# A hybrid RWKV-7 and NSA layer pair on one core: VectorE's and TensorE's order written down from the first key block to the last gate block

## The chip, the core and the metric

The kernel runs on one NeuronCore of a Trainium2 chip. The metric is device time in microseconds. Five engines have their own instruction streams: TensorE (PE, with its weight loads shown apart as PEld), VectorE (DVE), ScalarE (ACT), GpSimd (POOL) and SyncE (SP), which here only issues DMAs. Times are lower-is-better, and one measurement of this kernel spreads over about 0.2%.

## The reference, cut to what matters

The input is one sequence of 256 tokens with 2048 channels. The first layer is an RWKV-7 mixer, the second an NSA attention layer over a shared key/value projection; a last norm ends it. The change lies in the first layer, in the part that makes keys and gates and prepares the scan:

```python
mixed = u[None] + xx[None] * mu[:, None, None, :]
rkvz = jnp.einsum('nbtd,nde->nbte', mixed[:4], w_rkvz)
r, k, v, z = rkvz[0], rkvz[1], rkvz[2], rkvz[3]
...
decay = jnp.exp(-jnp.exp(w_log.astype(jnp.float32)))
a = jax.nn.sigmoid(a0 + (xa @ a1) @ a2)
kk = heads(k * k_k).astype(jnp.float32)
kk = kk / jnp.maximum(jnp.sqrt(jnp.sum(kk * kk, axis=-1, keepdims=True)), 1e-12)
k = k * (1.0 + (a - 1.0) * k_a)
...
o = wkv7_scan(rh, heads(decay), kh, vh, -kk, kk * ah.astype(jnp.float32))
...
o = (o + bonus.reshape(B, T, D)) * jax.nn.silu(z)
```

The kernel computes the scan in chunks of 64 tokens. For that it needs, per head and chunk, the inverse of a unit lower triangular 64x64 matrix, of which the two 32x32 diagonal blocks are inverted by VectorE (128 of them at once, one per partition, for half of the heads).

## The kernel before, in words

**Products in split precision.** Every weight piece of 512 columns is loaded by SyncE into `wraw`. ScalarE rounds it to the fp32r tile `whi` (`Weights.high`, line 211), VectorE makes the rest `wlo` as raw minus high (`Weights.low`, line 190). Activations are split in the same way into a high and a low half (`split_into`, lines 424 to 428). A product is then three matmuls: high by high, high by low, low by high. In a z block (`rows_step`, lines 577 to 590) one step over 128 input channels is one weight piece and six matmuls of 512 columns, three for each half of the tokens. In a k block (`cols_step`, lines 599 to 610) one weight piece serves four steps of three matmuls of 256 columns. There are five buffers for `whi` and `wlo` (`AHEAD + 2`): when the phase takes piece t, the split of piece t+3 is given, and its buffer is the one that the matmuls of piece t-2 have read.

**The stretch that the change touches.** `ZK` orders it: gate block z 0, sixteen key blocks k 0 to k 15 (`phase_k`), then gate blocks z 1 (`phase_z1`), z 2 and z 3 (`late_z`). After these comes the scan, in which all engines run in an order that a planner (`Deal`) lays out by costs and due times.

**Side stages of a k block.** After step 3 (`KP`) of block j, four small stages are given at once, each for a different earlier block: `k_close(j-3)`, `k_open(j)`, `k_turn(j-2)`, `k_norm(j-1)`. Each begins with a few TensorE products into PSUM: close has 16 small matmuls on `at` and `BK`, both in the tile `sp` (line 765); open has two on the loaded `w2s` (lines 705, 706); turn has two transposes of `rnx` (line 745); norm has four matmuls on the squares `sqk` (line 732). Behind the products come their readers: in close two ScalarE copies and three SyncE stores to `abd`; in open two tanh and a copy on ScalarE, the running sum `cum` on VectorE (line 712), exponentials on ScalarE and a product `an` on GpSimd (line 719); in turn `nk` and `at` on VectorE (lines 750, 751), four GpSimd products into `BK` (line 756) and the store to `spd`; in norm a maximum `sst` on VectorE (line 735), a power on GpSimd (line 736) and the copy `rnx` on ScalarE (line 738). At a block's end `k_square` squares and copies the block's result on ScalarE, and VectorE multiplies `f` (line 726). In z 1 the remaining stages are given after the steps 0, 6 and 12 (`ZP`).

**The inverse.** `stage_t(b)` runs in the background for two halves of the heads. It starts when `k_close(8b+7)` is given, loads the matrices back from `abd` into `invA` (line 812; on SyncE for b = 0, on GpSimd for b = 1), and then gives a serial chain of small VectorE operations (line 824): levels 2 and 4, then sixteen dots of level 8 (a multiply and a reduce each, with ScalarE transposes `Tt` ahead) and eight dots of level 16, then two stores. Half b = 1 begins only when half 0 is given in full. What is left of half 1 at the start of the scan is dealt there by the planner.

**How the order comes about.** The program's generators are interleaved by `Sched`: a phase yields costs, each adds to `sch.t`, and a background generator goes on when `sch.t` has passed the time that it asked for. A k step costs 327, a z step 1,280, and the side stages add their own sums to `sch.t` (720, 410, 215 and 500). The pauses in the inverse are times the factor 1.5 for b = 0 and 2 for b = 1. This gives an order of emission. Inside `tc.manual_schedule(engines=...)` the named engines keep it. All others are ordered by the framework's list scheduler, which takes the order of emission as a priority only and brings an instruction forward when it reckons that it is ready. Before the change, only TensorE keeps the order of emission, from k 0 to the end of z 1. In either case each engine's order is fixed when the program is built.

**The split of r.** After z 1 the sixteen tiles of r (`split_into(..., "r", k)`, VectorE at line 427) are made. So that ScalarE does not begin them early, their copy reads its scale from a one-element tile `gate` that GpSimd fills behind z 1.

Of the kernel before, what the change touches and what calls it, by code (L numbers as in the profile page):

```python
# [70 lines left out]
KPO = 3  # L71
KP, ZP = 3, (0, 6, 12)
AUX = {2: ("B0",), 3: ("G",), 4: ("B1",), 5: ("Y",), 7: ("A0",), 8: ("A1",), 9: ("T",)}
# [151 lines left out]
def hybrid_kernel(ctx: ExitStack, tc: tile.TileContext, a: dict, out: bass.AP):  # L225
# [197 lines left out]

    def split_into(src, nm, k, scale=1.0):
        h, l = ring(nm, k)
        S.activation(h, src, AF.Copy, scale=scale)  # L426
        V.tensor_tensor(l, src, h.bitcast(F32), op=OP.subtract)
        mixed[(nm, k)] = (h, l)
# [118 lines left out]
    def mixgen():  # L547
        for names in (("w", "a"), ("z",), ("k",), ("r",)):
            if names == ("r",):
                for k in range(NK):  # L550
                    x = xx[:, k, :]
                    V.scalar_tensor_tensor(x, x, MU[0][:, k:k + 1], xn[:, k, 1:], op0=OP.mult, op1=OP.add)
                    yield DR0
            for k in range(NK):
                for nm in names:
                    if not ring_free(nm):
                        yield lambda: ring_free(nm)
                    if nm in "wa":
                        while ("v", k) not in mixed:
                            yield 300.0  # L560
                    if nm == "r":
                        if k == 0:
                            yield lambda: "z1" in phase_done
                        split_into(xx[:, k, :], nm, k, gates[1.0])
                    else:
                        mix(nm, k)
                    yield {"w": DW, "a": DW, "k": DK, "z": DZ, "r": DRM}[nm]
        phase_done.add("mixed")
# [82 lines left out]

    gates = {}

    def gate(value):
        t = ph1.tile([128, 1], F32, name="gate", bufs=1)
        G.memset(t, value)
        gates[value] = t

    def close_z(nb, ps, ths, eng):
        for tt in range(2):  # L660
            th = ths[tt]
            S.activation(th, ps[tt], AF.Tanh, scale=gates[0.5] if nb == 1 else 0.5)
            S.activation(th, th, AF.Copy, scale=0.5, bias=0.5)
            V.tensor_tensor(th, ps[tt], th, op=OP.mult)
            store_heads(zd, nb, tt, th, eng)

    def phase_z(nb):
        ps = two()
        yield from rows_block(ps, "z", 512)
        close_z(nb, ps, [kph.tile([128, 512], F32, name="zth", bufs=2) for _ in range(2)], nc.sync)  # L670

# [23 lines left out]
    def k_open(j):  # L695
# [10 lines left out]
        PE.matmul(la[:, 256:], w2t[:, 1, sc:sc + 128], ha, start=True, stop=True)  # L706
        sch.t += 720
        thw, tha, cum = tmp("thw"), tmp("tha"), tmp("cum")
# [12 lines left out]
    def k_square(j, pk):  # L721
        k = KST[j]
        k["ksb"], k["sqk"] = [kph.tile([128, T], F32, name=n, bufs=2) for n in ("ksb", "t1")]
        S.activation(k["sqk"], pk, AF.Square, scale=KK[:, j:j + 1])
        S.activation(k["ksb"], pk, AF.Copy)
        V.tensor_tensor(k["f"], k["ksb"], k["f"], op=OP.mult)

    def k_norm(j):
        k = KST[j]
        k["rn"] = rn = accp("rn")  # L730
        for tt in range(2):
            PE.matmul(rn[:, 256 + 2 * tt:258 + 2 * tt], k["sqk"][:, tt * 128:(tt + 1) * 128], C("bo"), start=True, stop=True)
        sch.t += 410
        sst, rnt = [kph.tile([128, 2, 2], F32, name=n, bufs=2) for n in ("sst", "rnt")]
        V.tensor_scalar(sst, rn[:, 256:260].rearrange("p (a b) -> p a b", a=2), 1e-24, None, op0=OP.max)
        G.tensor_tensor(rnt, sst, half[:, 0:4].rearrange("p (a b) -> p a b", a=2), op=OP.pow)
        k["rnx"] = kph.tile([128, T], F32, name="rnx", bufs=2)
        S.activation(k["rnx"].rearrange("p (a b n) -> p a b n", a=2, b=2),
                     rnt[:, :, :, None].to_broadcast([128, 2, 2, 64]), AF.Copy)

    def k_turn(j):
        k = KST[j]
        rn, sp, an, f, pinv = [k[n] for n in ("rn", "sp", "an", "f", "pinv")]
        for tt in range(2):
            PE.transpose(rn[:, tt * 128:(tt + 1) * 128], k["rnx"][:, tt * 128:(tt + 1) * 128], ident)
        sch.t += 215
        k["BK"] = BK = sp[:, 0:512].rearrange("p (c x t) -> p c x t", c=NCH, x=2)
        k["at"] = at = sp[:, SPW - 256:]
# [10 lines left out]
    def k_close(j):  # L759
        k = KST.pop(j)  # L760
        ab, cd = accp("ab"), accp("ab")
        for c in range(NCH):
            for h in range(2):
                r, o = [slice(64 * i, 64 * i + 64) for i in (h, h ^ (c % 2))]
                PE.matmul((ab, cd)[c % 2][o, c // 2 * 64:c // 2 * 64 + 64], c3(k["at"])[r, c, :], k["BK"][r, c, h, :], start=True, stop=True)
        sch.t += 500
        abs_ = k["abs"] if j < 2 else kph.tile([128, T], F32, name="abs", bufs=2)
        S.activation(abs_[:, 0:128], ab[:, 0:128], AF.Copy)
        S.activation(abs_[:, 128:256], cd[:, 0:128], AF.Copy)
        for c, src, dst in ((0, 0, 0), (2, 0, 64), (2, 64, 0)):  # L770
            n = 64 if c else 128
            nc.sync.dma_start(abd[j, c:c + 2, :, dst:dst + n].rearrange("c k p s -> p (c k) s"),
                              abs_[src:src + n, 64 * c:64 * c + 128].rearrange("p (n s) -> p n s", s=32))
        a1done.add(j)

    def phase_k(j):
# [3 lines left out]
        for q in range(4):  # L780
            for s, cost in enumerate(cols_step(o, "k", q)):
                yield cost
                n = 4 * q + s
                if n == KP:
                    for lag, part in ((3, k_close), (0, k_open), (2, k_turn), (1, k_norm)):
                        if j >= lag:
                            part(j - lag)
            if j == NK - 1:
                used.update(("k", k) for k in range(4 * q, 4 * q + 4))
        k_square(j, o)  # L790

    def phase_z1():
        banks(acc=(2, 3, 0, 1))
        gate(0.5)
        ps = two()
        for k in range(NK):
            yield from rows_step(ps, "z", k, W.get(), 512)
            if k in ZP:
                for lag, part in ((3, k_close), (2, k_turn), (1, k_norm)):
                    j = NK + ZP.index(k) - lag  # L800
                    if j < NK:
                        part(j)
        close_z(1, ps, [kph.tile([128, 512], F32, name="zth", bufs=2) for _ in range(2)], nc.sync)
        gate(1.0)
        phase_done.add("z1")
# [87 lines left out]
    def stage_t(b):  # L893
        yield lambda: (8 * b + 7) in a1done
        A = inverse_load(b)
        if b:
            yield lambda: 0 in tdone
        yield 3000.0 if b else 9000.0
        left = inverse_ops(b, A)
# [34 lines left out]
    def late_z(nb):  # L934
        nonlocal A10, T00, vt, zt
        ps = two()
        for k in range(NK):
            yield from rows_step(ps, "z", k, W.get(), 512)
            if nb == 3:
                used.add(("z", k))  # L940
# [4 lines left out]
            elif k == ZHOOK[0]:  # L945
# [11 lines left out]
                for t in (A10, T00, Yb[0]):  # L957
                    G.memset(t, 0.0)
        close_z(nb, ps, [t.rearrange("p x c d -> p (x c d)") for t in (vt, zt)], G)

# [5 lines left out]
    for nm, i in ZK:  # L966
        if (nm, i) == ("k", 0):
            ordered.enter_context(tc.manual_schedule(engines={PE.engine}))
        sch.run((late_z(i) if i > 1 else phase_z1() if i else phase_z(i)) if nm == "z" else phase_k(i))
        if (nm, i) == ("z", 1):  # L970
            ordered.close()
    phase_done.update(("z", "k"))
# [1071 lines left out]
```

## Time and profile before

| | |
|---|---|
| median of 3 runs | 1145.12 us |
| lowest and highest | 1143.18 and 1145.2 us |
| the profiled execution | 1146.2 us |
| its span, first to last instruction | 1144.4 us |
| mean granted TensorE clock | 0.989 |

The profiled execution's own time is 1.8 us more than its span, for what lies around it, and 1.1 us above the median. In the profile "busy" of TensorE counts from a matmul's start to a modelled end, so that pipelined matmuls overlap; how fast they go is read from the distance of their starts. A line of the timeline gives a start, a duration, the engine, the line of the kernel, the operation with written and read tiles, and how many instructions were merged; in square brackets stands the idle time before it and what ended it.

### The profile page before, as it was taken

Reading aid. Unit: us, or ns where it says so; the run is one execution under the profiler, and the core shown is the slowest. Engines: PE = TensorE matmul, PEld = TensorE weight load, DVE = VectorE, ACT = ScalarE, POOL = GpSimd, SP = SyncE. Lnnn points to the kernel's source line nnn. Section 1 sums busy time; section 2 is a strip of 40 time slices with the busy share of each in tenths; the row PEclk is TensorE's granted clock in tenths of the full one; section 3 lists DMA queues with packets and bytes.
Section 4 is the critical chain, followed back from the end, with each engine's and each line's share of the span. In section 5 each row is a group of like instructions: output and inputs, shape, how many; then the busy total and the mean of one; then the engine's idle time right before and its main releaser. Section 6 shows DMA issues by size and latency. Waiting matters only on the chain.

```text
span 1144.4 us, 24519 instructions
## 1 busy us (share of the span) xinstructions
PE 1107.3 (97%) x8880; PEld 939.5 (82%) x8880; DVE 869.0 (76%) x1806; ACT 716.1 (63%) x1696; POOL 367.2 (32%) x465
## 2 busy tenths in 40 slices
PE   8999999998999999999999999999999999999996
PEld 7778899987778777777778878787889988898786
DVE  6999976689786997768666876674576888988564
ACT  5667688866745456566556766564656666666553
POOL 1400057766252556653010010100333435352212
PEclk9999999998989999999999999999999999999999
DMA  6558878876898958864457758585656453848552
GB/s 218 174 190 236 247 203 256 241 219 208 245 271 255 237 159 247 211 171 134 131 179 234 225 164 284 160 292 167 188 148 162 122 146 102 203 114 278 164 186 106
DMA packets 239033, 225.35 MB, mean 197 GB/s; under 512 B 58053, under 2 KB 185333, under 8 KB 238912
## 3 DMA queue, kind: packets, MB, share of 16 engines
q1 hardware_dynamic: 233472, 216.65, 64.5%
q0 software_dynamic: 5440, 7.14, 2.4%
q8 instruction: 70, 1.15, 0.5%
q14 instruction: 51, 0.42, 0.1%
HBM read 200.48 MB, written 23.10 MB: 195 GB/s over the span
## 4 chain that ended last, share of the span: by engine, by line
PE 77%; DVE 9%; DMA 4%; issue 4%; POOL 3%; ACT 2%; SPq 0%; ACTq 0%; POOLq 0%; DVEq 0%
PE bank L587 12%; PE bank L589 12%; PE bank L586 12%; PE bank L1337 5%; PE bank L611 5%; DVE wlo L190 3%; PE bank L612 3%; PE bank L241 2%; PE bank L605 2%; PE bank L606 2%; PE bank L607 2%; PE bank L1340 2%; PE pair L1359 2%; PE pair L1361 1%; PE pair L1360 1%
## 5 line engine op out<-in xcount | busy, mean ns | idle before, releaser
L190 DVE TENSOR_TENSOR wlo<-wraw,whi 128x512 fp32r<-128x512 f32 (+2 forms) x616 | 447.3, 741 | 162.4 <-ACT whi L211 159.4
L211 ACT ACTIVATE whi<-wraw 128x512 fp32r<-128x512 f32 (+2 forms) x664 | 401.3, 620 | 241.4 <-PE bank L589 93.0
L587 PE MATMUL bank<-wlo,mx 128*128 128x512 f32 (+3 forms) x576 | 217.4, 379 | 7.4 <-DVE wlo L190 6.5
L589 PE MATMUL bank<-whi,mx 128*128 128x512 f32 (+3 forms) x576 | 215.6, 377 | 0.0
L586 PE MATMUL bank<-whi,mx 128*128 128x512 f32 (+3 forms) x576 | 187.9, 379 | 2.1 <-ACT mx L426 0.9
L587 PEld LDWEIGHTS bank<-wlo,mx 128*128 128x128 f32 x576 | 109.4, 190 | 26.2 <-DVE wlo L190 8.5
L586 PEld LDWEIGHTS bank<-whi,mx 128*128 128x128 f32 x576 | 108.4, 190 | 20.0 <-ACT whi L211 1.5
L589 PEld LDWEIGHTS bank<-whi,mx 128*128 128x128 f32 x576 | 109.3, 190 | 16.7 <-POOL mx L1926 0.4
L1337 PE MATMUL bank<-mx,whi 128*128 128x512 f32 x256 | 102.1, 430 | 0.0
L190 POOL TENSOR_TENSOR wlo<-wraw,whi 128x512 fp32r<-128x512 f32 (+2 forms) x48 | 63.0, 1314 | 110.8 <-ACT whi L211 90.1
L611 PE MATMUL bank<-mx,whi 128*128 128x512 f32 x240 | 86.6, 397 | 0.0
L605 PE MATMUL bank<-mx,whi 128*128 128x256 f32 (+1 forms) x288 | 83.0, 288 | 0.3 <-ACT mx L426 0.3
L606 PE MATMUL bank<-mx,whi 128*128 128x256 f32 (+1 forms) x288 | 81.4, 283 | 0.0
L607 PE MATMUL bank<-mx,wlo 128*128 128x256 f32 (+1 forms) x288 | 81.3, 282 | 0.0
L587 PE MATMUL bank<-wlo,kvh 128*128 128x512 f32 x192 | 76.9, 401 | 0.0
L589 PE MATMUL bank<-whi,kvl 128*128 128x512 f32 x192 | 76.1, 396 | 0.0
L612 PE MATMUL bank<-mx,wlo 128*128 128x256 f32 x256 | 70.6, 285 | 0.2 <-DVE wlo L190 0.2
L1340 PE MATMUL bank<-mx,wlo 128*128 128x256 f32 x256 | 70.7, 284 | 0.0
L586 PE MATMUL bank<-whi,kvh 128*128 128x512 f32 x192 | 67.4, 396 | 0.0
L1337 PEld LDWEIGHTS bank<-mx,whi 128*128 128x128 f32 x256 | 48.0, 189 | 10.6
L605 PEld LDWEIGHTS bank<-mx,whi 128*128 128x128 f32 (+1 forms) x288 | 54.2, 188 | 1.3 <-ACT mx L426 0.7
L607 PEld LDWEIGHTS bank<-mx,wlo 128*128 128x128 f32 (+1 forms) x288 | 54.2, 188 | 0.8 <-DVE wlo L190 0.2
(350 smaller groups left out, 2301.9 us busy)
## 6 DMA issues: line engine op xcount, KB each, us to landing
wraw<-in_a_w_rkvz_dram SPq DMA_DIRECT2D x128, 512.0 KB, 5.2
wraw<-in_kv_w_dram SPq DMA_DIRECT2D x48, 512.0 KB, 4.5
wraw<-in_b_w_in_dram SPq DMA_DIRECT2D x40, 512.0 KB, 4.3
wraw<-in_a_w_o_dram SPq DMA_DIRECT2D x32, 512.0 KB, 4.6
wraw<-in_b_w_o_dram SPq DMA_DIRECT2D x32, 512.0 KB, 4.1
spd<-sp SPq DMA_DIRECT2D x16, 642.0 KB, 5.4
wraw<-in_b_w_in_dram SPq DMA_DIRECT2D x24, 384.0 KB, 3.3
spl<-spd SPq DMA_DIRECT2D x14, 642.0 KB, 7.2
```

What stands on the lines that cost most here:

```text
L190: eng.tensor_tensor(lv, src, hv.bitcast(F32), op=OP.subtract)
L211: self.nc.scalar.activation(hv, src, AF.Copy)
L586: PE.matmul(o, mh[:, ts], wh[:, 0, :], start=k == ends[0], stop=False)
L587: PE.matmul(o, mh[:, ts], wl[:, 0, :], start=False, stop=False)
L589: PE.matmul(o, ml[:, ts], wh[:, 0, :], start=False, stop=k == ends[1])
L605: PE.matmul(o, wh[:, s, :], mh, start=k == 0 and first, stop=False, **kw)
L606: PE.matmul(o, wh[:, s, :], ml, start=False, stop=False, **kw)
L607: PE.matmul(o, wl[:, s, :], mh, start=False, stop=k == NK - 1, **kw)
L611: PE.matmul(o, wh[:, s, :], joint[nm, k], start=k == 0, stop=False, **kw)
L612: PE.matmul(o[:, :T], wl[:, s, :], mh, start=False, stop=False, **kw)
L1337: both = lambda: PE.matmul(o, wh[:, s, :], joint["r", k], start=k == 0, stop=k == NK - 1)
L1340: PE.matmul(o[:, :T], wl[:, s, :], mixed["r", k][0], start=False, stop=False)
```

## The change

From k 0 to the end of z 3, TensorE and VectorE both keep the order of emission (before: TensorE alone, and only to the end of z 1). Each side stage becomes a generator with a `yield` between its products and their readers. The products are given after step 3 as before (`begin_parts`), the readers after step 11 (`KS8`, `end_parts`); in z 1 the readers follow their products by two steps. VectorE's multiply of `f` moves from `k_square` to the readers of `k_norm`, one block later. The closing multiply and stores of gate blocks 1 and 2 are given after step 1 (`ZREST`) of the next gate block. The pause between the load and the first operation of half 1 of the inverse goes from 3,000 to 8,000. The sums that open and norm add to `sch.t` go from 720 to 860 and from 410 to 500. The `gate` tile goes.

```diff
-KP, ZP = 3, (0, 6, 12)
+KP, KS8, ZP, ZREST = 3, 11, (0, 6, 12), 1
...
-        S.activation(h, src, AF.Copy, scale=scale)
+        S.activation(h, src, AF.Copy)
...
     def close_z(nb, ps, ths, eng):
         for tt in range(2):
             th = ths[tt]
-            S.activation(th, ps[tt], AF.Tanh, scale=gates[0.5] if nb == 1 else 0.5)
+            S.activation(th, ps[tt], AF.Tanh, scale=0.5)
             S.activation(th, th, AF.Copy, scale=0.5, bias=0.5)
-            V.tensor_tensor(th, ps[tt], th, op=OP.mult)
-            store_heads(zd, nb, tt, th, eng)
+
+        def rest():
+            for tt in range(2):
+                V.tensor_tensor(ths[tt], ps[tt], ths[tt], op=OP.mult)
+                store_heads(zd, nb, tt, ths[tt], eng)
+        return rest
...
-        sch.t += 720
+        sch.t += 860
+        yield
         thw, tha, cum = tmp("thw"), tmp("tha"), tmp("cum")
...
         S.activation(k["ksb"], pk, AF.Copy)
-        V.tensor_tensor(k["f"], k["ksb"], k["f"], op=OP.mult)
...
-        sch.t += 410
+        sch.t += 500
+        yield
         sst, rnt = [kph.tile([128, 2, 2], F32, name=n, bufs=2) for n in ("sst", "rnt")]
+        V.tensor_tensor(k["f"], k["ksb"], k["f"], op=OP.mult)
...
         sch.t += 215
+        yield
...
         sch.t += 500
+        yield
...
+    begun = []
+
+    def begin_parts(j, parts):
+        begun.extend(part(j - lag) for lag, part in parts if 0 <= j - lag < NK)
+        for p in begun:
+            next(p)
+
+    def end_parts():
+        for p in begun:
+            for _ in p:
+                pass
+        begun.clear()
...
                 if n == KP:
-                    for lag, part in ((3, k_close), (0, k_open), (2, k_turn), (1, k_norm)):
-                        if j >= lag:
-                            part(j - lag)
+                    begin_parts(j, ((3, k_close), (0, k_open), (2, k_turn), (1, k_norm)))
+                elif n == KS8:
+                    end_parts()
...
             if k in ZP:
-                for lag, part in ((3, k_close), (2, k_turn), (1, k_norm)):
-                    j = NK + ZP.index(k) - lag
-                    if j < NK:
-                        part(j)
-        close_z(1, ps, [kph.tile([128, 512], F32, name="zth", bufs=2) for _ in range(2)], nc.sync)
-        gate(1.0)
+                begin_parts(NK + ZP.index(k), ((3, k_close), (2, k_turn), (1, k_norm)))
+            elif k - 2 in ZP:
+                end_parts()
+        zrest.append(close_z(1, ps, [kph.tile([128, 512], F32, name="zth", bufs=2) for _ in range(2)], nc.sync))
...
-        yield 3000.0 if b else 9000.0
+        yield 8000.0 if b else 9000.0
...
             yield from rows_step(ps, "z", k, W.get(), 512)
+            if k == ZREST:
+                zrest.pop()()
...
-        close_z(nb, ps, [t.rearrange("p x c d -> p (x c d)") for t in (vt, zt)], G)
+        zrest.append(close_z(nb, ps, [t.rearrange("p x c d -> p (x c d)") for t in (vt, zt)], G))
+        if nb == 3:
+            zrest.pop()()
...
-            ordered.enter_context(tc.manual_schedule(engines={PE.engine}))
+            ordered.enter_context(tc.manual_schedule(engines={PE.engine, V.engine}))
...
-        if (nm, i) == ("z", 1):
-            ordered.close()
+    ordered.close()
```

More of the change, by code (lines that the diff above doesn't have):

```diff
@@ L422, in ring_free, with split_into @@
         return len(o) < NK or o[-NK] in used or o[-NK][0] in phase_done
-    def split_into(src, nm, k, scale=1.0):
+    def split_into(src, nm, k):
         h, l = ring(nm, k)
-        S.activation(h, src, AF.Copy, scale=scale)
+        S.activation(h, src, AF.Copy)
         V.tensor_tensor(l, src, h.bitcast(F32), op=OP.subtract)
@@ L563, in mixgen @@
                             yield lambda: "z1" in phase_done
-                        split_into(xx[:, k, :], nm, k, gates[1.0])
+                        split_into(xx[:, k, :], nm, k)
                     else:
@@ L650, in hybrid_kernel @@
     ha = consts.tile([LORA, T], F32, name="ha")
[L652 to L657, printed above, removed]
     def close_z(nb, ps, ths, eng):
@@ L669, in phase_z @@
         yield from rows_block(ps, "z", 512)
-        close_z(nb, ps, [kph.tile([128, 512], F32, name="zth", bufs=2) for _ in range(2)], nc.sync)
+        close_z(nb, ps, [kph.tile([128, 512], F32, name="zth", bufs=2) for _ in range(2)], nc.sync)()
     sch.run(phase_v())
@@ L790, in phase_k @@
         k_square(j, o)
+    zrest = []
     def phase_z1():
         banks(acc=(2, 3, 0, 1))
-        gate(0.5)
         ps = two()
```

## The prediction

> **What bounds the kernel now.** The page's busy times come first.
>
> ```profile
> PE 1107.3 (97%) x8880; PEld 939.5 (82%) x8880; DVE 869.0 (76%) x1806; ACT 716.1 (63%) x1696; POOL 367.2 (32%) x465
> ```
>
> TensorE sets the time, so what an order can win is time in which TensorE stands or runs slowly. The busy times by stage, cut at the side stages of blocks 3 and 11, the start of z 1, the end of z 1 and the end of z 3:
>
> ```profile
> core 0: us, PE busy (x) PEld busy (x) DVE busy (x) ACT busy (x) POOL busy (x), PEclk, DMA share, GB/s
> 165.60:228.59 62.99, 62.99 (x594) 60.17 (x593) 41.38 (x73) 52.76 (x139) 45.61 (x56) 1.00 0.86 239
> 228.59:272.84 44.25, 40.44 (x360) 36.31 (x360) 39.40 (x97) 30.40 (x83) 25.86 (x31) 1.00 0.73 213
> 272.84:303.10 30.26, 27.36 (x154) 21.48 (x153) 28.11 (x42) 16.65 (x36) 12.20 (x13) 0.89 0.70 207
> 303.10:354.18 51.08, 45.99 (x195) 37.27 (x193) 37.03 (x95) 30.94 (x59) 19.60 (x39) 0.93 0.94 268
> ```
>
> In the first row TensorE never stands and VectorE works 66%. In the next three VectorE is at 89%, 93% and 72%, and TensorE has holes and a lower clock. TensorE's timeline and its waits:
>
> ```profile
> 165.60 0.46 PE L765 MATMUL bank<-sp 64*64 64x64 f32 x16
> 167.54 0.36 PE L605 MATMUL bank<-mx,whi 128*128 128x256 f32 x1
> 228.59 0.46 PE L765 MATMUL bank<-sp 64*64 64x64 f32 x16
> 265.32 0.46 PE L765 MATMUL bank<-sp 64*64 64x64 f32 x16
> 272.84 0.40 PE L586 MATMUL bank<-whi,mx 128*128 128x512 f32 x1
> 276.33 0.46 PE L765 MATMUL bank<-sp 64*64 64x64 f32 x16 [1.95 <-DVE sp L751]
> 279.31 0.77 PE L586 MATMUL bank<-whi,mx 128*128 128x512 f32 x1
> 283.66 0.40 PE L587 MATMUL bank<-wlo,mx 128*128 128x512 f32 x1
> 298.63 0.46 PE L765 MATMUL bank<-sp 64*64 64x64 f32 x16
> 317.38 0.80 PE L587 MATMUL bank<-wlo,mx 128*128 128x512 f32 x1 [4.77 <-DVE wlo L190]
> ```
> ```profile
> 320.96:354.18 33.22, 33.22 (x148) 1.00 0.91 246
> ```
> ```profile
> PE bank L587 <- DVE wlo L190: 4.8, 1, 4.8
> PE bank L765 <- DVE sp L751: 2.0, 1, 2.0
> PE bank L765 <- POOL sp L756: 1.7, 3, 0.9
> ```
>
> The loss against an undisturbed pace, stage by stage:
> - Blocks 3 to 11 take (228.59 - 165.60)/8 = 7.87 us each. From block 11's side stage to block 15's are 36.73 us against 4 x 7.87 = 31.50: **5.2 lost**.
> - From there to z 1 are 7.52 us. A side stage takes 167.54 - 165.60 = 1.94, so a block's 48 matmuls go at (7.87 - 1.94)/48 = 0.12. A period less four steps (twelve of these) is 6.4: **1.1 lost**.
> - The 148 matmuls of the last row run at 33.22/147 = 0.226 us, a z step of six at 1.36 us. Z 1's row holds 95 of them (21.5 us) and three smaller side stages (together 2.3 us, an estimate from those 1.94) in 30.26: **6.4 lost**, of which 4.35 - 10 x 0.226 = 2.1 are the slow matmuls from 279.31 to 283.66.
> - Z 2 and z 3 hold 194 in 51.08 us, 43.8 undisturbed: **7.2 lost**.
>
> Together 19.9 us. Why VectorE was late, from its timeline:
>
> ```profile
> 168.20 0.47 DVE L750 SCALAR_TENSOR_TENSOR nk<-ksb,par,bank 128x256 f32<-128x256 f32 x1
> 169.10 0.68 DVE L712 TENSOR_TENSOR_SCAN cum<-cst,thw 128x256 f32<-128x256 f32 x1
> 234.83 0.18 DVE L824 COPY invT<-invA 128x16 f32<-128x16 f32 x1 [4.07 <-DMA invA<-abd]
> 305.75 1.28 DVE L664 TENSOR_TENSOR zth<-bank,zth 128x512 f32<-128x512 f32 x2
> 307.54 3.83 DVE L427 TENSOR_TENSOR mx<-xx,mx 128x256 fp32r<-128x256 f32 x10
> 316.01 0.18 DVE L824 COPY invT<-invA 128x16 f32<-128x16 f32 x1 [4.64 <-DMA invA<-abd]
> ```
>
> Twice VectorE stands for the load of the inverse, 4.07 and 4.64 us, with `wlo` and `nk` queued behind; before the second, ten splits of r ran in one burst. Between 234.83 and z 1's end it works through half 0.
>
> **The change, part by part.** I counted the order of emission by the kernel's own costs (327 a k step, 2,075 at a side stage, 1,280 a z step).
>
> *The two stands.* Half 0's load is given at step 12 of block 10; 9,000 later, its first read comes at step 4 of block 12. Block 12's side stage is due at 228.59 + 7.87 = 236.46, and VectorE runs about one piece ahead, as the five buffers let it, so it arrives near 236.5. The data lay ready at 234.83. For half 1 the chain of waits shows:
>
> ```profile
> 302.94 5.16 DMA abd<-abs
> 309.26 6.63 DMA invA<-abd
> ```
>
> From the last side stage (298.63) to the data (316.01) are 17.4 us. In the new order that side stage follows z 1's step 12, and the read falls at z 2's step 14, since half 1 waits for half 0 and then 8,000: 18 steps, 24.4 us. Both stands go, with 2 and 7 us to spare; if the cover fails, they cost what they cost now. What is late next is VectorE's own work.
>
> *Blocks 12 to 15.* VectorE needs 41.38/8 = 5.17 of 7.87 us. Half 0's operations come on top:
>
> ```profile
> 228.59:272.84 44.25, 20.37 (x57) 1.21 (x3) 0.00 (x0) 1.00 0.73 213
> ```
> ```profile
> L824 DVE MEMSET invT<- x2: 85/498/912, 1.3 to 2.3; 128x1024 f32 x1, 128x32 f32 x1
> ```
> ```profile
> 276.71 1.21 DVE L824 TENSOR_REDUCE invM<-invX 128x64 f32<-128x1024 f32 x1
> 277.84 0.68 DVE L190 TENSOR_TENSOR wlo<-wraw,whi 128x512 fp32r<-128x512 f32 x1
> 278.44 0.68 DVE L824 TENSOR_TENSOR invX<-invA,invM 128x512 f32<-128x512 f32 x1
> 279.05 0.68 DVE L190 TENSOR_TENSOR wlo<-wraw,whi 128x512 fp32r<-128x512 f32 x1
> ```
>
> Without three large ones of level 16 (1.21 each, as the first of the four rows) they take 0.31 us apiece. The plan puts 8, 14, 9 and 8 of them into blocks 12 to 15, and the clearing of `invT`, which ran unneeded early at 1.3 us, now takes 0.91 in block 12. VectorE needs 8.6, 9.5, 8.0 and 7.7 us: an excess of about 2.4, plus an estimated 1 for ScalarE's transposes that it now stands for. Part hides in the slack of the side stages. I take **2.0** of 0 to 5.2 (as now).
>
> *Z 1's first side stage.* Its products need readers given at step 11 of block 15; between lie four k steps (1.44) and one z step, 2.8 us, where before 12 k steps lay between. Behind VectorE's readers come two products on POOL:
>
> ```profile
> 169.14 1.99 POOL L756 TENSOR_TENSOR sp<-nk,an 64x256 f32<-64x256 f32 x2
> ```
>
> `cum`, `nk` and `at` take 1.5 by VectorE's rows above, the products 2.0: 3.5 in all, with the excess on top. I take a wait of 1.5 and the slow clock (2.1): **3.6**, of 0 to 6.4.
>
> *The pile of level 16.* Eight dots of level 16 are given one per z step, from z 1's step 11 to z 2's step 2. By the starts of the four rows above, a large operation takes 1.13, a small 0.61, `wlo` 0.60; a dot is two operations, and the order is two large dots, four small, two large. From z 1's step 11, up to the `wlo` that z 2's step 5 needs, stand seven dots (3 x 2.26 + 4 x 1.22 = 11.7), seven `wlo` (4.2), two splits of r (0.8) and the postponed multiplies of z 1 (1.28): 17.9 us. TensorE gets there after 10 steps and a side stage, 14.0: it waits 3.9. The eighth dot and one more `wlo` (2.9) against one step of 1.36 add 1.5. Together 5.4. Whether the clock follows:
>
> ```profile
> 458.82 0.46 PE L1130 MATMUL pair<-S,ars 64*64 64x64 f32 x16 [2.29 <-DVE mv L1169]
> ```
> ```profile
> 460.00:464.00 4.00, 4.00 (x24) 2.99 (x25) 2.86 (x3) 3.04 (x8) 3.36 (x7) 0.63 1.17 186
> ```
>
> A stand of 2.29 us was followed by a clock of 0.63. I add 2.1: **7.5**, of 0 (had the list scheduler's spread stayed) to 9.
>
> [...]
>
> *The rest.* In z 3, half 1's small operations, splits of r and z 2's multiplies need some 13 us in seven steps of 1.36 (seven `wlo` 4.2, nineteen small operations 5.9, five splits 1.9, the multiplies 1.3), which the three pieces of lead (4.1) nearly hold: 0.5, of 0 to 4. Half 1 enters the scan with three dots more (six operations of 0.3, 1.8 us of VectorE): 0.5, of -1 to 2. At nothing: the `gate` fills and TensorE's written order in z 2 and z 3 (z 1 already runs so, at the same pitch); `f` one block later (its first reader, POOL's product, comes a block after); SyncE's stores, two steps or eight k steps later, whose data the scan alone needs, and half 0's load above.
>
> **Sum:** 2.0 + 3.6 + 7.5 + 1.0 = 14.1 lost after, 19.9 before: 5.8 won. The profiled execution's 1146.2 becomes 1140.4; against the median, 1.1 lower, **1139.3**.
>
> **The rivals.** *All holes close.* Against it: VectorE works 39.40 + 28.11 + 37.03 = 104.5 us in these stages, and TensorE undisturbed needs 125.6 - 19.9 = 105.7; VectorE would have to be busy without a pause, yet block 11 alone leaves it 2.7 idle. For it: two of the holes are stands for a DMA. Some 16 won: 1129.
>
> *The waits only move.* VectorE remains the bound of blocks 12 to 15 (5.2) and z 1's side stage (6.4), and the pile comes new (7.5): 19.1 + 1.0, no gain, 1145.
>
> *The written order stalls every k block.* It hangs on when VectorE gets `thw`:
>
> ```profile
> 168.39 0.43 ACT L711 ACTIVATE thw<-thw 128x256 f32<-128x256 f32 x1
> ```
>
> Before, VectorE took `nk` at 168.20 and `cum` last; written, `cum` stands ahead, from 168.9, when its input `thw` is there, to 169.5, and `nk` comes 1.3 later. Behind `nk` and POOL's two products:
>
> ```profile
> 172.68 0.42 ACT L738 ACTIVATE rnx<-rnt 128x256 f32<-128x256 f32 x1 [1.10 <-POOL rnt L736]
> ```
> ```profile
> 174.83 0.38 PE L745 MATMUL bank<-cst,rnx 128*128 128x128 f32 x2
> ```
>
> From the end of `rnx` (173.1) to its reader lie 1.7 us; 0.4 are left. If POOL takes one more product of 1.0 ahead of the power and ScalarE one rounding of 0.6, each of 13 blocks waits 1.2: 15.6, less the 2.0 that blocks 12 to 15 then don't lose. That is 7.8 slower, 1153. It decides from 0.45 a block. [...] Against it: VectorE idles 34% there.
>
> That the order does nothing new is excluded by bursts like the ten splits.
>
> **How the numbers follow.** Forecast 0.58 (its own range 1133 to 1143), all holes close 0.12, waits move 0.13, every block stalls 0.17. About 0.2% (2.3 us) is what a measurement can tell. Faster 0.70, same 0.13, slower 0.17. The range, 1129 to 1148, takes in the first rival and the second and leaves out most of the third.
>
> **What would show it.** Right: no idle before the copy of `invA` in VectorE's rows; block 12 to 15 periods near 8.4; level-16 dots between z 1's step 11 and z 2's step 4, with `wlo` ending waits of about 4 us there. Wrong: side stages of blocks 3 to 10 with waits for POOL, or periods over 8.3 there; a stand for the load of half 1; no waits around the pile.

## The result

The change makes the kernel about 1% slower: 1156.22 us in the median of 4 runs (1154.57 to 1158.33), beside 1144.72 us for the kernel before (4 runs, 1143.18 to 1145.2). The ratio is 1.0104, with a 95% interval from 1.008 to 1.0127. Single executions spread more than the first runs of before suggested (in 23 later ones it took 1141.16 to 1148.91 us), so the experiments below are compared by their ratios to before and the intervals of these. Two executions at a much lower granted clock, one of before (1373.31 us at 0.727) and one in the last experiment (1210.22 us at 0.846), stay out of all ratios. The profiled execution of after is the lowest of its four (1154.57 us, span 1152.4, mean clock 0.991), that of before lies above its median (1146.2, span 1144.4). The two traces thus differ by 8.0 us, the medians by 11.5, and the trace accounts below are for the 8.0.

The page's busy times say nothing of it: TensorE is as busy as before to within 1.3 us.

```profile
PE 1108.6 (96%) x8880; PEld 937.9 (81%) x8880; DVE 883.5 (77%) x1806; ACT 716.3 (62%) x1696; POOL 370.5 (32%) x463
```

The stages do, cut as before at the side stages of blocks 3 and 11, the start of z 1, its end after 96 matmuls, and the end of z 3 (columns as in the prediction: busy times of PE, PEld, DVE, ACT, POOL, then the granted clock):

```profile
164.79:238.25 73.46, 65.98 (x593) 60.96 (x592) 57.82 (x84) 53.82 (x138) 49.26 (x57) 0.98 0.76 214
238.25:285.54 47.29, 41.69 (x359) 38.77 (x359) 38.37 (x84) 34.87 (x93) 29.10 (x34) 0.93 0.66 196
285.54:312.30 26.76, 24.73 (x155) 19.73 (x154) 24.13 (x45) 16.20 (x37) 10.09 (x11) 1.00 0.73 225
312.30:363.51 51.21, 47.05 (x192) 35.96 (x192) 43.81 (x100) 25.94 (x46) 21.59 (x40) 0.97 0.85 245
```

Blocks 3 to 11, where TensorE never stood before, take 73.46 us in place of 62.99: 9.18 a block in place of 7.87. That is 10.5 us lost in the one stage where there had been nothing to win. (Seven of the eight blocks have a wait, 7.5 us in all; each of these blocks takes another 0.2 beyond wait and period, and one of them 1.7, at a lower clock that the last section shows.) The next row loses another 3.0 (47.29 against 44.25). Z 1 wins 3.5 (26.76 against 30.26), z 2 and z 3 are even, and the rest of the program is 1.3 shorter. Block 3 began 0.8 earlier.

What TensorE and VectorE wait for between 160 and 365 us (us in total, times, the longest), from the waits of after:

```profile
PE bank L744 <- ACT rnx L737: 15.1, 12, 2.0
PE bank L587 <- DVE wlo L190: 3.9, 3, 2.9
DVE cum L710 <- ACT thw L709: 18.1, 12, 2.4
```

The first line is new. Twelve times TensorE stands before the transposes of `rnx` (L744 here, L745 before). VectorE stands twelve times before `cum`, and nothing waits any more for the load of the inverse on VectorE. The timeline shows one turn of what goes round, from one `rnx` to the next, in order of time:

```profile
203.65 0.41 ACT L737 ACTIVATE rnx<-rnt 128x256 f32<-128x256 f32 x1 [1.54 <-POOL rnt L735]
203.97 0.46 ACT L707 ACTIVATE thw<-bank,par 128x256 f32<-128x256 f32 x1
204.12 0.44 PE L744 MATMUL bank<-cst,rnx 128*128 128x128 f32 x2 [1.44 <-ACT rnx L737]
204.68 0.41 ACT L709 ACTIVATE thw<-thw 128x256 f32<-128x256 f32 x1
205.13 0.69 DVE L710 TENSOR_TENSOR_SCAN cum<-cst,thw 128x256 f32<-128x256 f32 x1 [1.38 <-ACT thw L709]
205.74 0.45 DVE L750 SCALAR_TENSOR_TENSOR nk<-ksb,par,bank 128x256 f32<-128x256 f32 x1
206.27 1.87 POOL L756 TENSOR_TENSOR sp<-nk,an 64x256 f32<-64x256 f32 x2 [2.29 <-DVE nk L750]
206.57 0.97 DVE L733 TENSOR_TENSOR f<-ksb,f 128x256 f32<-128x256 f32 x1
207.47 0.15 DVE L734 TENSOR_SCALAR sst<-bank 128x4 f32<-128x4 f32 x1
208.22 1.07 POOL L717 TENSOR_TENSOR an<-an,pinv 128x256 f32<-128x256 f32 x1
209.25 2.32 POOL L756 TENSOR_TENSOR sp<-f,pinv 64x256 f32<-64x256 f32 x2
211.65 1.07 POOL L735 TENSOR_TENSOR rnt<-sst,half 128x4 f32<-128x4 f32 x1
212.75 0.42 ACT L737 ACTIVATE rnx<-rnt 128x256 f32<-128x256 f32 x1 [1.10 <-POOL rnt L735]
```

Read it by starts, each released by the line named. ScalarE waits for the power, makes `rnx`, and only behind it `thw` (1.03 to its last piece). VectorE's `cum` follows after 0.45, `nk` after 0.61, the two `nk` products on GpSimd after 0.53. Then GpSimd works without a pause: those products 1.95, `an` 1.03, the two `f` products 2.40, the power. From its start 1.10 pass to the next `rnx`. Together 9.10 us: a loop, closed through the fixed orders of three engines, and longer than the 7.87 that TensorE needs for a block. `sst` was ready at 207.6, but the power that reads it starts at 211.65, behind the `f` products.

So what happened is the third rival's case, a written order that stalls the k blocks. By the stages, k blocks and the way to z 1 are 13.5 us longer, all from z 1 to the end is 4.7 shorter, and the start 0.8: 8.0.

### The profile page after: what moved, and what is told of

It reads as the page before. It is cut to its first block, busy times and chain, and to the rows that moved or that the text cites. A ratio compares the mean times of both kernels' runs of the same rounds, so it can differ in the third digit from the quotient of the medians.

```text
span 1152.4 us, 24563 instructions
## 1 busy us (share of the span) xinstructions
PE 1108.6 (96%) x8880; PEld 937.9 (81%) x8880; DVE 883.5 (77%) x1806; ACT 716.3 (62%) x1696; POOL 370.5 (32%) x463
## 3 DMA queue, kind: packets, MB, share of 16 engines
q8 instruction: 70, 1.15, 0.4%
## 4 chain that ended last, share of the span: by engine, by line
PE 71%; DVE 12%; POOL 4%; ACT 4%; issue 4%; DMA 4%; ACTq 0%; SPq 0%; POOLq 0%; DVEq 0%
PE bank L587 12%; PE bank L589 12%; PE bank L586 11%; PE bank L1353 5%; DVE wlo L190 4%; PE bank L611 4%; POOL sp L756 2%; PE bank L1356 2%; PE bank L612 2%; PE bank L241 2%; PE bank L605 2%; PE bank L606 2%; PE pair L1375 1%; PE bank L607 1%; PE pair L1377 1%
## 5 line engine op out<-in xcount | busy, mean ns | idle before, releaser
L190 DVE TENSOR_TENSOR wlo<-wraw,whi 128x512 fp32r<-128x512 f32 (+2 forms) x616 | 453.0, 750 | 139.9 <-ACT whi L211 138.3
L587 PEld LDWEIGHTS bank<-wlo,mx 128*128 128x128 f32 x576 | 108.6, 189 | 27.7 <-DVE wlo L190 10.5
L605 PE MATMUL bank<-mx,whi 128*128 128x256 f32 (+1 forms) x288 | 85.0, 295 | 0.3 <-ACT mx L426 0.3
L606 PE MATMUL bank<-mx,whi 128*128 128x256 f32 (+1 forms) x288 | 83.4, 290 | 0.0
L605 PEld LDWEIGHTS bank<-mx,whi 128*128 128x128 f32 (+1 forms) x288 | 56.2, 195 | 1.3 <-ACT mx L426 0.7
L606 PEld LDWEIGHTS bank<-mx,whi 128*128 128x128 f32 (+1 forms) x288 | 56.3, 195 | 0.5
```

The source lines that it names most:

```text
L190: eng.tensor_tensor(lv, src, hv.bitcast(F32), op=OP.subtract)
L587: PE.matmul(o, mh[:, ts], wl[:, 0, :], start=False, stop=False)
L605: PE.matmul(o, wh[:, s, :], mh, start=k == 0 and first, stop=False, **kw)
L606: PE.matmul(o, wh[:, s, :], ml, start=False, stop=False, **kw)
```

## The experiments

The theory: a serial loop (`rnx`, `thw`, `cum`, `nk`, GpSimd's products, the power) of 9.1 us sets the pace of a k block. `cum` ahead of `nk`, and the `f` products ahead of the power, are the two pieces that make it too long. Rivals: the readers come too late in the block (step 11); or it costs by itself to hold VectorE in a written order; or an engine's sum of work is the bound. All edits are to the kernel after the change.

### `f` back to the block's end

```diff
         S.activation(k["ksb"], pk, AF.Copy)
+        V.tensor_tensor(k["f"], k["ksb"], k["f"], op=OP.mult)
...
-        V.tensor_tensor(k["f"], k["ksb"], k["f"], op=OP.mult)
```

> VectorE's multiply of f goes back from the readers of k_norm to the end of k_square; all else as after the change. Theory A, the serial loop: in every k block rnx, then ScalarE's thw behind it, then cum, nk, POOL's two nk products, an, two f products and the power, then the next rnx hang on one another and take 9.1 us, more than TensorE's 7.87. Without the two f products (2.1 us) between an and the power, the loop is 7.0 us, so TensorE's waits for rnx in blocks 3 to 11 go, the period there is 7.9, and the time falls to 1139 to 1144. Theory B, the late giving: the readers come too late because they are given at step 11; moving f changes nothing, the period stays over 9.0, the time 1153 to 1159.

Measured: 1142.22 us (1140.69 to 1145.23), ratio to before 0.9989, interval 0.9975 to 1.0003. Blocks 3 to 11:

```profile
165.12:229.80 64.68, 63.81 (x593) 59.58 (x593) 50.05 (x84) 51.82 (x136) 45.52 (x58) 1.00 0.85 242
```

The order of GpSimd is now the two `nk` products (202.88), `an` (205.12), the power (205.81), and only then the `f` products (206.97). The waits for `rnx` fall from 15.1 us to 3.2. The time is where the theory of the loop put it; the period is 8.1, not the 7.9 expected. By the two ratios (1.0104 and 0.9989) the place of one VectorE instruction is worth some 13 us.

### `cum` last

```diff
-        for p in begun:
+        for p in sorted(begun, key=lambda p: p.__name__ == "k_open"):
```

> The readers are given in the order close, turn, norm, open, so that VectorE's cum stands behind nk, f and sst; the products keep their order. Theory A: nk no longer hangs on thw, the loop is rnx, transposes, nk, POOL's four products and the power, 6.6 us, below 7.87: no waits for rnx, period 7.9 in blocks 3 to 11, time 1139 to 1145. Theory B: still given at step 11, so the period stays over 9.0 and the time 1153 to 1159.

Measured: 1145.7 us (1142.8 to 1148.39), ratio 1.0009, interval 0.9992 to 1.0027; blocks 3 to 11 take 65.6 us (165.96 to 231.60), the waits for `rnx` sum to 5.0. The `f` products still stand ahead of the power, but `nk` no longer waits for `thw`. The time is just above the 1139 to 1145 expected, and some waits stay where none were expected. Either cut shortens the turn: from one power on GpSimd to the next it is 8.1 us with `f` back (197.71 to 205.81) and 8.3 with `cum` last (189.42 to 197.74). Both are still somewhat over the period, and neither kernel comes quite back to 62.99.

### Readers after step 7

```diff
-KP, KS8, ZP, ZREST = 3, 11, (0, 6, 12), 1
+KP, KS8, ZP, ZREST = 3, 7, (0, 6, 12), 1
```

> The readers are given after step 7 instead of step 11, one weight piece earlier, in the same order. Theory B: the chain starts one piece (1.4 us) earlier and the waits for rnx (1.3 us a block) go, time 1140 to 1146. Theory A: VectorE already stands for thw when it gets to the readers, so nothing starts earlier: period 9.0 to 9.3 in blocks 3 to 11 and a time of 1153 to 1159.

Measured: 1157.5 us (1156.14 to 1161.93), ratio 1.0134, interval 1.0102 to 1.0166. The waits for `rnx` are 15.7 us, those of `cum` for `thw` 21.3 (18.1 in after, in the same stretch). Readers four steps earlier don't make anything earlier: the loop goes round at its own pace, and VectorE only stands longer for its input. That the readers come too late is ruled out as the cause.

### VectorE not held

```diff
-            ordered.enter_context(tc.manual_schedule(engines={PE.engine, V.engine}))
+            ordered.enter_context(tc.manual_schedule(engines={PE.engine}))
```

> Only TensorE keeps the order of emission up to the end of z 3, VectorE is ordered by the list scheduler as before the change; the two-part stages, f one block later and the pause of 8,000 stay. Theory A: the list scheduler brings nk ahead of cum, the loop does not form, period 7.9 in blocks 3 to 10, and the time is that of before or a little less, 1140 to 1146. Theory B: the readers are given late for VectorE here too, period over 8.5, time over 1150.

Measured: 1142.88 us (1140.08 to 1146.48), ratio 0.9986, interval 0.9971 to 1.0002. The windows and the waits of VectorE:

```profile
164.80:227.78 62.98, 62.98 (x593) 60.16 (x592) 41.61 (x73) 53.24 (x139) 46.48 (x56) 1.00 0.87 240
```
```profile
DVE invT L837 <- DMA invA<-abd: 8.2, 2, 5.0
```

With all the rest of the change kept, and `f` late too, the blocks run at 7.87 again; the list scheduler gives `f` ahead of `nk`, and GpSimd takes the `f` products while it waits for `nk`. The loop thus needs VectorE's written order. Both stands for the inverse's load are back, 8.2 us.

### `f` back and `cum` last together

> The kernel after the change with two edits at once: the multiply f goes back to the end of the same block, and the readers of k_open are given last of the four stages, so that cum stands behind nk in VectorE's order. Alone, the first gave 1142.2 us and 64.7 us for blocks 3 to 11, the second 1145.7 and 65.6. Serial loop: with both, neither cum nor the f products lie between one rnx and the next; the loop is nk 0.45, two nk products 2.0, the power 1.4, rnx 0.4 and its transposes, far under 7.87, so blocks 3 to 11 go back to 63.0 us (7.87 a block) and the time is about 1139 to 1141. Rival (to hold VectorE in a written order costs by itself, whatever the order): blocks 3 to 11 stay at 64.5 or more, and the time at 1142 or more.

Both edits above at once. Measured: 1158.31 us (1157.41 to 1159.97), ratio 1.0118, interval 1.0099 to 1.0137. The theory's 1139 to 1141 missed by 17 us: the side stages of blocks 3 to 11 are 9.2 us apart. The rival's bounds hold, but its reason does not, as the next kernel shows. Two edits that each won 10 us and more lose all of it together. The timeline shows why:

```profile
203.61 0.42 ACT L737 ACTIVATE rnx<-rnt 128x256 f32<-128x256 f32 x1 [0.70 <-POOL rnt L735]
...
204.81 0.37 ACT L723 ACTIVATE ksb<-bank 128x256 f32<-128x256 f32 x1
205.21 0.42 DVE L724 TENSOR_TENSOR f<-ksb,f 128x256 f32<-128x256 f32 x1 [2.50 <-ACT ksb L723]
...
209.17 0.47 DVE L750 SCALAR_TENSOR_TENSOR nk<-ksb,par,bank 128x256 f32<-128x256 f32 x1
209.72 2.06 POOL L756 TENSOR_TENSOR sp<-nk,an 64x256 f32<-64x256 f32 x2 [1.85 <-DVE nk L750]
211.86 1.33 POOL L735 TENSOR_TENSOR rnt<-sst,half 128x4 f32<-128x4 f32 x1
213.23 0.41 ACT L737 ACTIVATE rnx<-rnt 128x256 f32<-128x256 f32 x1 [0.71 <-POOL rnt L735]
```

This is another loop, in this turn of 9.62 us; it is read from the trace, and no run takes it apart. ScalarE's order, which the list scheduler made, here has `rnx` ahead of the block's squares and `ksb`. With `f` back alone it was the other way round (squares 197.03, `ksb` 197.38, `rnx` 198.75), so `f` did not depend on `rnx`. Now `f` waits for `ksb` and so for `rnx`; VectorE stands 2.50 us, and behind `f` five pieces of other work (three `wlo`, two `xx`, 3.6 us to `nk`'s start) are queued ahead of `nk`. From `nk` the way is short. A change in VectorE's order thus came with another one in ScalarE's, which nobody wrote.

### `sst` ahead of `f`

```diff
+        V.tensor_scalar(sst, rn[:, 256:260].rearrange("p (a b) -> p a b", a=2), 1e-24, None, op0=OP.max)
         V.tensor_tensor(k["f"], k["ksb"], k["f"], op=OP.mult)
-        V.tensor_scalar(sst, rn[:, 256:260].rearrange("p (a b) -> p a b", a=2), 1e-24, None, op0=OP.max)
```

> The kernel after the change with one pair of lines swapped: in the readers of k_norm, sst is given ahead of the multiply f. f stays one block later than before, so VectorE's work and the waits for ksb are as after the change; but GpSimd's fixed order now has the power ahead of the two f products. Serial loop through GpSimd: the f products (2.06 us) and f (0.5) leave the loop of 9.1, which falls under 7.87; blocks 3 to 11 at 63.5 to 65 us and the time about 1142. Rival (it is the late place of f on VectorE that costs, through readers that come late for the block): blocks 3 to 11 stay at about 73 us, the time about 1155.

Measured: 1142.73 us (1141.93 to 1147.04), ratio 0.999, interval 0.9978 to 1.0002. GpSimd's timeline (it ends within the `f` products) and the window of blocks 3 to 11:

```profile
201.35 1.87 POOL L756 TENSOR_TENSOR sp<-nk,an 64x256 f32<-64x256 f32 x2 [1.01 <-DVE nk L750]
203.29 1.07 POOL L717 TENSOR_TENSOR an<-an,pinv 128x256 f32<-128x256 f32 x1
204.33 1.45 POOL L735 TENSOR_TENSOR rnt<-sst,half 128x4 f32<-128x4 f32 x1
205.75 0.74 POOL L756 TENSOR_TENSOR sp<-f,pinv 64x256 f32<-64x256 f32 x1
```
```profile
165.80:228.79 62.99, 62.99 (x594) 60.15 (x593) 56.71 (x83) 52.60 (x137) 46.07 (x56) 1.00 0.85 239
```

Two lines swapped, everything else as in the change: the power stands ahead of the `f` products, TensorE waits for no `rnx` from block 3 to block 11, and the blocks are back to 7.87. VectorE is as busy as after the change (56.71 against 57.82 us). So it was neither its work nor the late place of `f` as such, but the place of the `f` products ahead of the power.

### `rnx` written twice

```diff
+        S.activation(k["rnx"].rearrange("p (a b n) -> p a b n", a=2, b=2),
+                     rnt[:, :, :, None].to_broadcast([128, 2, 2, 64]), AF.Copy)
```

> The kernel after the change, with ScalarE's copy rnx (0.41 us) written twice in a row; one is superfluous. Serial loop: the second copy lies in the loop, so each block with a wait gets longer by about 0.41: blocks 3 to 11 from 73.46 to about 76.7 us, twelve blocks 4.9 us, the time about 1161. Rival (the blocks are limited by the sum of an engine's work, VectorE's 57.8 or POOL's 49.3 of 73.5 us busy, and not by a loop): ScalarE is busy 53.8 of 73.5 us there, the copy finds room, and the time stays at about 1156.

Measured: 1162.72 us (1158.93 to 1164.51), ratio 1.0154, interval 1.0131 to 1.0177. ScalarE's timeline:

```profile
195.89 0.41 ACT L737 ACTIVATE rnx<-rnt 128x256 f32<-128x256 f32 x1 [1.38 <-POOL rnt L735]
196.22 0.26 ACT L772 ACTIVATE abs<-bank 128x128 f32<-128x128 f32 x1
196.37 0.41 ACT L739 ACTIVATE rnx<-rnt 128x256 f32<-128x256 f32 x1
...
205.49 0.41 ACT L737 ACTIVATE rnx<-rnt 128x256 f32<-128x256 f32 x1 [1.31 <-POOL rnt L735]
```

The second copy ends the pair 0.48 later (the list scheduler put a copy of `abs` between the two), and the turn takes 9.60 in place of 9.10, though ScalarE has room (56.42 us busy of the 78.40): the loop sets the pace, and no engine's sum of work. Blocks 3 to 11 take 78.4 us, 1.7 more than the 76.7 expected; the clock there is 0.93 in place of 0.98.

### Level-16 dots spread

On the kernel with both edits, the pause behind each level-16 instruction of half 0 is doubled:

```diff
-                   pause=DT * (0.75 if hb == 8 else 1.0))
+                   pause=DT * ((0.75 if b else 1.5) if hb == 8 else 1.0))
```

> As the kernel with f back and cum last, and the level-16 dots of half 0 of the inverse are given one every two z steps (pause of 1.5 in place of 0.75), from z 1's step 11 to about z 2's step 10. The pile is a price of its own: the waits of TensorE for wlo in z 1's end and z 2's start (3.9 to 4.5 us) and the slow clock behind them go, 4 to 7 us less than without the spread: about 1134 to 1136. Rival (given back): half 1 begins eight z steps later, some eight more of its dots enter the scan or pile up in z 3, and the time is within 1.5 us of the one without the spread.

Measured: 1154.59 us (1152.44 to 1155.87) beside 1158.31 on the same chip, 3.7 less; ratio to before 1.0086, interval 1.0069 to 1.0103. (The level expected, 1134 to 1136, was lost with the second loop; the difference of 4 to 7 is just missed.) The waits for `wlo` fall from 5.2 to 1.9 us. The same on the kernel with `sst` first:

> The kernel with sst ahead of f (1142.7 us, no loop), and in it the level-16 dots of half 0 one every two z steps. The pile has its own price: TensorE's waits for wlo at z 1's end and z 2's start (0.59 + 2.86 + 1.32 without the spread) and the slow clock behind them go, 3.5 to 5 us, as the spread won 3.7 on the kernel with the other loop; about 1138 to 1139. Rival (half 1, eight z steps later, gives it back in z 3 or the scan, and the 3.7 was the clock of a kernel full of holes): 1141.5 or more.

Measured: 1141.93 us (1140.53 to 1145.22), ratio 0.9974, interval 0.996 to 0.9987, beside 0.999 without the spread: some 1.8 us by the ratios, where 3.5 to 5 were expected; the time lies within the rival's bound (1141.5 or more). The waits for `wlo` at the pile fell as they should, from 0.59 + 2.86 + 1.32 to 0.97 + 0.92. From z 1's start to the scan's it is 4.0 us shorter (77.8 against 81.8), and from there to the end 5.1 longer (793.3 against 788.2). Half 1 begins later, 31 multiplies of it in place of 26 are left for the scan, and its results come later to `Yb`, for which TensorE waits 3.7 us in the scan in place of 1.5. The rest of the 5.1 was not followed. The profiled execution (2.0 us above its kernel's median) gives all of it back there; by the ratios something may be left, but the intervals overlap.

### Z 1's side stages two steps later

```diff
-KP, KS8, ZP, ZREST = 3, 11, (0, 6, 12), 1
+KP, KS8, ZP, ZREST = 3, 11, (2, 7, 12), 1
```

With `sst` first and the spread:

> As the kernel with sst ahead of f and the spread, and z 1's three side stages after its steps 2, 7 and 12 in place of 0, 6 and 12. The wait of TensorE at z 1's first side stage (4.09 us for rnx in the kernel with sst ahead of f) is a matter of distance to block 15's readers: two z steps (2.8 us) later it falls to about 1.3, and with less slow clock behind it the time is 2.5 to 4 us under that of the kernel without this move, about 1135. Rival (ScalarE's queue sets when rnx is written, behind roundings that wait for TensorE's own z steps, so that rnx moves along): the wait stays at 3 or more and the time within 1 us.

Measured: 1139.97 us (1138.19 to 1141.19), ratio 0.9948, interval 0.9931 to 0.9965. The wait at z 1's first side stage is

```profile
275.49 0.44 PE L744 MATMUL bank<-cst,rnx 128*128 128x128 f32 x2 [1.43 <-ACT rnx L737]
```

in place of 4.13: as the theory of distance had it. The time fell by 2.0, less than the 2.5 to 4 expected. This version is 0.5% faster than the kernel before, the largest gain of all these versions. Without the spread:

> The kernel with sst ahead of f (1142.7 us) and z 1's three side stages after its steps 2, 7 and 12; the level-16 dots as the change has them, without the spread. With the spread as well it was 1140.0 us. If the spread is given back in the scan (with it TensorE waited there 3.4 to 3.7 us for Yb, without it 1.5, and the kernel with sst first won only 0.8 us by it), the time here is 1139 to 1141.5, with waits for wlo of 4 to 5 us at the pile and one of about 1.4 for rnx in z 1, and the scan 788 to 789 us long in place of 792. Rival (the spread and the move only work together, since the postponed side stages pile up with the level-16 dots): a wait for wlo of over 4 us in one piece, and 1142.5 or more.

Measured: 1141.2 us (1138.42 to 1144.81), ratio 0.9972, interval 0.9955 to 0.9989, with waits for `wlo` of 5.0 in all at the pile (the longest 2.88), 1.39 for `rnx` in z 1, and 790.3 us from the scan's start, where 788 to 789 were expected. The intervals of the two versions overlap: what the spread is worth beside the move, 2.7 us by the ratios, isn't settled by them.

### Readers right behind their products

```diff
                     begin_parts(j, ((3, k_close), (0, k_open), (2, k_turn), (1, k_norm)))
-                elif n == KS8:
                     end_parts()
...
-            elif k - 2 in ZP:
                 end_parts()
```

> The kernel with sst ahead of f, but the readers of all side stages are given right behind their products (after step 3, and in z 1 after the steps 0, 6 and 12) and not eight k steps or two z steps later; VectorE still keeps the written order. Theory (the order within the stages matters, the distance matters little while three pieces of wlo lie ready): VectorE stands for TensorE's products once a block, within its 2.7 us of slack; blocks 3 to 11 at 63 to 64 us; in z 1 the first side stage no longer waits for rnx (4.09), and the time is 1139 to 1143. Rival (the two parts are what makes a written order bearable): VectorE's stand comes through to wlo, blocks 3 to 11 take 66 us or more, and the time is 1146 or more.

Measured, with `sst` first: 1148.29 us (1145.11 to 1151.6), ratio 1.0028, interval 1.0011 to 1.0045. Each side got a part. Blocks 3 to 11 take 63.48 us, as the theory had it, but the time is in the rival's bounds, and z 1's first side stage still waits 2.31 us for `rnx` where the theory had no wait. From block 11 to block 15 it is 40.0 us (228.64 to 268.67) where the kernel in two parts needs 34.4 (228.79 to 263.21). So the two parts are worth some 6 us in these two traces (4.4 by the ratios 1.0028 and 0.999), nearly all of it in the blocks where the inverse comes on top of VectorE's work.

## Why the prediction was wrong

**The step that failed** is the one line of costs "at nothing": "`f` one block later (its first reader, POOL's product, comes a block after)". That looks at who needs the data, and the data was in time. It doesn't look at the order of GpSimd, which the list scheduler derives anew and then keeps: before, GpSimd took the `f` products while it waited for `nk` (written from 191.53), almost off the chain:

```profile
190.32 1.90 POOL L756 TENSOR_TENSOR sp<-f,pinv 64x256 f32<-64x256 f32 x2 [1.44 <-DVE f L726]
192.45 1.99 POOL L756 TENSOR_TENSOR sp<-nk,an 64x256 f32<-64x256 f32 x2
```

With `f` given behind `nk` they stand between the `nk` products and the power, 2.4 us of the 9.1. So the steady blocks, costed at nothing, lost 10.5. The prediction's own sign of being wrong, periods over 8.3 in blocks 3 to 10, came true with 9.18. With `sst` ahead of `f` and nothing else changed, the loss is gone. But the 5.8 us that were forecast don't come in full even then: that kernel's ratio is 0.999, about 1 us, and its trace is 3.9 us shorter than that of before (1140.5 against 1144.4). By stages, the traces win 2.6 from block 11 to z 1 (44.25 - 41.69; 4.3 by the sum's terms), lose 0.5 from z 1 to the scan (81.83 - 81.34; 1.5 won by the terms) and win 2.0 behind it.

**The third rival came nearest.** It had `cum` ahead of `nk`, `thw` as its input, and a wait for `rnx` once a block. Beside its 15.6 us of waits stand 15.1 in twelve; beside its 7.8 us stand 8.0 in the traces and 11.5 in the medians. That the sizes agree so well is in part luck: it used up a slack of 0.4 us in each block and did not have the link that closes the loop, `thw` behind `rnx` on ScalarE. What it let GpSimd take ahead of the power was one product, not the two of `f`, and the rounding that it put on ScalarE wasn't needed. It got 0.17 for a bad reason: "VectorE idles 34% there". The share of idle time does not tell whether a loop is too long. In the kernel with `sst` first VectorE is busy 90% of the same stage (56.71 of 62.99) and TensorE never stands.

**The two stands** are gone, as predicted. What that is worth was overrated: the kernel with VectorE free has them back, and its ratio is that of the kernel with a written order and no loop (0.9986 and 0.999). Both wait some 4 us at z 1's first side stage (4.01 and 4.09). From block 11 to z 1 the written order is 1.5 us shorter (41.69 against 43.20), and from z 1 to the scan, where it has waits of 4.8 at the pile, 1.1 us longer (81.83 against 80.78).

**Blocks 12 to 15**: after lost 8.5 (40.02 - 31.50). In the kernel with `sst` first, without the loop, it is 34.42 - 31.50 = 2.9, beside the predicted 2.0 of 0 to 5.2. For an order without a loop the term was about right.

**Z 1's side stage and the pile** came where they were put:

```profile
289.52 0.44 PE L744 MATMUL bank<-cst,rnx 128*128 128x128 f32 x2 [2.04 <-ACT rnx L737]
304.83 1.22 DVE L837 TENSOR_TENSOR invX<-invA,invM 128x1024 f32<-128x1024 f32 x1
318.97 0.50 PE L587 MATMUL bank<-wlo,mx 128*128 128x512 f32 x1 [0.59 <-DVE wlo L190]
323.49 0.80 PE L587 MATMUL bank<-wlo,mx 128*128 128x512 f32 x1 [2.88 <-DVE wlo L190]
324.61 1.22 DVE L837 TENSOR_REDUCE invT<-invX 128x64 f32<-128x1024 f32 x1
```
```profile
323.00:326.00 3.00, 2.51 (x6) 1.82 (x6) 2.97 (x4) 0.14 (x1) 0.00 (x0) 0.50 0.72 150
```

The first level-16 instruction starts at 304.83, in z 1's step 11, and the last at 324.61, in z 2. The waits are 3.5 us (predicted 5.4), and the clock reads 0.50 behind the longer one, as assumed. Z 1's first side stage waits 2.04 (predicted 1.5; without the loop, in the kernel with `sst` first, it is 4.09, so the term was too small there), and z 1 as a whole lost 26.76 - 21.5 - 2.3 = 3.0 (predicted 3.6). From z 1 on, the change won 4.7 us (1.5 by the sum's terms), so in after these terms were too dark; they weren't what failed.

## What to carry to other kernels

A written order on one engine is a promise about all others: where the remaining engines are ordered by a scheduler, look at their order too, follow the chain from one block's reader round to the next block's, and add it up. Here that sum was over the block's period, and neither VectorE's idle share nor readers four steps earlier helped; one instruction's place did. Two cures of one loop can make another when put together, so the chain is summed again for each version.

## What the hardware showed

**Some VectorE operations took longer beside GpSimd's products.** In blocks 3 to 11, by shape, before and after (busy us, mean ns):

```profile
L190 DVE TENSOR_TENSOR wlo<-wraw,whi 128x512 fp32r<-128x512 f32 x33 | 27.0, 837 | 22.6 <-ACT whi L211 21.9
L726 DVE TENSOR_TENSOR f<-ksb,f 128x256 f32<-128x256 f32 x8 | 3.4, 426 | 0.0
```
```profile
L190 DVE TENSOR_TENSOR wlo<-wraw,whi 128x512 fp32r<-128x512 f32 x34 | 33.9, 1011 | 3.0 <-ACT whi L211 2.7
L733 DVE TENSOR_TENSOR f<-ksb,f 128x256 f32<-128x256 f32 x8 | 7.7, 964 | 0.0
```

The same `f` took 0.43 us in before, with GpSimd idle, and 0.96 in after, beside the `nk` products. Held in order, VectorE has more of its work beside GpSimd's products (`wlo` takes 1.01 us in the mean in place of 0.84), and its busy time per block rises from 5.2 to 7.2 us (57.82/8); ten operations on `xx` (7.1 us), which the list scheduler had done before 146 us, are among it. Yet before, with two `f` products on GpSimd from 190.32 to 192.22, one of two neighbours took longer and the other did not (with GpSimd idle `wlo` took 0.69 in before at 196.97, and `nk` 0.46 in after at 196.63):

```profile
190.33 1.28 DVE L190 TENSOR_TENSOR wlo<-wraw,whi 128x512 fp32r<-128x512 f32 x1
191.53 0.47 DVE L750 SCALAR_TENSOR_TENSOR nk<-ksb,par,bank 128x256 f32<-128x256 f32 x1
```

`wlo` reads two tiles, `nk` one tile and a bank. The operation alone does not tell the two apart: `xx`, the same operation as `nk` but with two tiles, took longer too, here in the kernel with `f` back, beside the `f` products on GpSimd (198.69 to 200.28) and after them:

```profile
198.74 0.95 DVE L552 SCALAR_TENSOR_TENSOR xx<-xx,prm,xn 128x256 f32<-128x256 f32 x1
200.75 0.47 DVE L552 SCALAR_TENSOR_TENSOR xx<-xx,prm,xn 128x256 f32<-128x256 f32 x1
```

So in these rows it goes with the operands. Not in every row: `cum`, which also reads two tiles, took 0.68 in before at 192.42, 0.03 ahead of the `nk` products, and 0.69 in after at 205.13, with GpSimd idle; with both edits (`f` back and `cum` last) it took 1.15 at 210.09, 0.37 behind the start of those products. What makes these operations longer is not shown here.

**The clock fell after a stand of 1.02 us and after two of 0.35 and 0.44, and not after one of 1.44.** In after, TensorE stood 1.02 us up to 185.22, and then the clock fell. In the kernel with both edits (`f` back and `cum` last) it fell after two stands of only 0.35 us up to 204.08 and 0.44 up to 204.96. The windows behind the two:

```profile
188.00:190.00 2.00, 2.00 (x12) 2.00 (x12) 1.66 (x3) 1.03 (x2) 1.85 (x3) 0.54 0.73 210
```
```profile
205.50:208.60 3.10, 3.10 (x16) 3.10 (x16) 3.10 (x6) 3.10 (x10) 2.02 (x3) 0.50 0.29 89
```

In after a matmul took 0.21 us in place of 0.12 up to 189.8. That block lasted 10.62 us, 1.7 more than period and wait. The next took 7.87 without a wait, so that the two together are only 0.3 us over two turns of the loop. Behind the longer stand of 1.44 up to 204.12 the clock stayed at 1.00 (204 to 208). What decides is not shown here.
